# Two gates of a gated block as eight pairs of weight tiles by seven products, results through DRAM

## The chip, the cores and the metric

One Trainium2 chip; the kernel runs on one of its cores. The metric is the device time of one execution in microseconds (us). The core has a matmul engine (PE), a vector engine (DVE), a scalar engine (ACT), a general engine (POOL) and a queue engine (SP) that issues most DMAs. Each runs its own instructions in order, and they wait for each other by semaphores.

## The reference

The input x has 1024 tokens of 1024 channels. All matrices are float32.

```python
h = rmsnorm(x, norm_g)
xa, za, ub, gb, zb, g_a, g_b = split(h @ w_in)          # seven sections of 1024 channels
# first branch: short conv, chunkwise matrix memory with 4 heads, normalization, skip
ya = ((ha + skip_a * xc) * silu(za)) @ w_proj_a
# second branch: 31-tap causal conv, layer norm over channels
c = causal_depthwise_conv(ub * sigmoid(gb), conv_b_w, conv_b_b)
c = standardize(c) * ln_b_g + ln_b_b
yb = (silu(c) * silu(zb)) @ w_pw2 + b_pw2
x = x + (sigmoid(g_a) * ya + sigmoid(g_b) * yb) @ w_out
ple_gate = sigmoid(rmsnorm(x, ple_norm_g) @ w_ple_gate)
return rmsnorm(x + (p @ w_ple) * ple_gate, final_g)
```

## The kernel before

Channels lie on the 128 partitions, tokens on the free axis, so a product is made per output tile: 128 channels by 1024 tokens. Every float32 operand is split exactly into a high part (a cast by ACT to a 22-bit-like format, `split`, line 87) and a low part (the difference, by DVE or POOL, line 88). A product of two operands takes three matmuls: high x high, high x low, low x high. `gemm` (lines 209 to 222) makes one output tile: 8 blocks of the contraction x 2 halves of the tokens x 3 = 48 matmuls of a 128x128 weight and 128x512 moving columns, into one PSUM buffer of the pool `pg` (two buffers, tiles `g`). The other small results use `pm` (four banks, tiles `m`).

Weights come as a stream in a fixed order (`order`, class `Stream`): tile `wr` is loaded by SP into a single buffer, its parts `wh` and `wl` are made by ACT and DVE one tile ahead, with two buffers each. `h` lies in four buffers of the pool `hp` (high and low part of each token half). Long-lived tiles use the pool `sp` (20 buffers, tiles `s`), short ones `zp` (3) and `vp` (4).

The order of the work: p @ w_ple and the rmsnorm; the x section with its short conv; four heads, each with two tiles of za and a chunkwise recurrence; then, for eight tiles t, the first gate's section (`GA + t`) and the first branch's projection (`proj`, t), whose result waits in DRAM (`ma_d`). The long conv of the second branch (31 taps on DVE, line 350) is made of eight tiles, whose taps are drained beside all this in small numbers; each needs two tiles of `in` (sections GB and UB), and its result waits in DRAM (`c_d`). Then six tiles of the second gate (section GBT), the layer norm's sums (lines 636 to 665), two more gate tiles, and eight tiles of the value gate (section ZB), with the activation of the layer norm (`second_act`) two tiles behind. At last the second projection (`pw2`), the merge, and `out` and `gate` by token halves.

Each engine's order is set by a list scheduler when the kernel is built; on the chip the order is fixed.

## Time and profile before

| | |
|---|---|
| time, median of 3 runs | 1172.83 us (1172.17 to 1173.25) |
| profiled execution: span from first to last instruction | 1169.3 us |
| PE matmul busy | 1147.2 us, 98% |
| DVE busy | 817.7 us, 70% |
| ACT busy | 400.4 us, 34% |
| POOL busy | 33.0 us, 3% |
| chain that ended last | PE 93%, DVE 4% |

The span is one profiled execution; the runs' times are some 3.5 us longer, since they hold what lies around it. An engine's busy share says how much of the span it worked, not whether the end waited for it: that is read from the waits of PE and from the chain.

### The profile page before, as it was taken

Reading aid. Unit: us, or ns where it says so; the run is one execution under the profiler, and the core shown is the slowest. Engines: PE = TensorE matmul, PEld = TensorE weight load, DVE = VectorE, ACT = ScalarE, POOL = GpSimd, SP = SyncE. Lnnn points to the kernel's source line nnn. Section 1 sums busy time; section 2 is a strip of 40 time slices with the busy share of each in tenths; the row PEclk is TensorE's granted clock in tenths of the full one; section 3 lists DMA queues with packets and bytes.
Section 4 is the critical chain, followed back from the end, with each engine's and each line's share of the span. In section 5 each row is a group of like instructions: output and inputs, shape, how many; then the busy total and the mean of one; then the engine's idle time right before and its main releaser. Section 6 shows DMA issues by size and latency. Waiting matters only on the chain.

```text
span 1169.3 us, 13098 instructions
## 1 busy us (share of the span) xinstructions
PE 1147.2 (98%) x5276; PEld 929.8 (80%) x5276; DVE 817.7 (70%) x1113; ACT 400.4 (34%) x540; POOL 33.0 (3%) x67
## 2 busy tenths in 40 slices
PE   7999999999999999999999999999999999999996
PEld 5777777778787887888888888888888888888885
DVE  5929989869984699828769999365334545466875
ACT  7633323642525343221111111147232212334542
POOL 1400000000000000000000000000000000000000
PEclk9999999999999999999999999999999999999998
DMA  9311121201011011221211233211113229422232
GB/s 328 133 36 36 38 72 36 71 20 55 19 62 47 19 55 37 72 91 42 102 54 55 108 105 112 90 54 36 55 36 108 90 73 387 152 87 94 91 127 72
DMA packets 29660, 98.18 MB, mean 84 GB/s; under 512 B 3148, under 2 KB 5340, under 8 KB 29600
## 3 DMA queue, kind: packets, MB, share of 16 engines
q1 hardware_dynamic: 25344, 82.37, 20.5%
q0 software_dynamic: 4256, 14.98, 3.3%
q8 instruction: 41, 0.67, 0.2%
q14 instruction: 19, 0.16, 0.0%
HBM read 80.55 MB, written 16.79 MB: 83 GB/s over the span
## 4 chain that ended last, share of the span: by engine, by line
PE 93%; DVE 4%; ACT 1%; DMA 1%; issue 0%; SPq 0%; DVEq 0%; ACTq 0%
PE g L221 21%; PE g L217 21%; PE g L218 21%; PE g L235 5%; PE g L234 5%; PE g L236 5%; PE m L548 2%; PE m L561 2%; PE m L535 1%; PE m L403 1%; PE m L555 1%; PE m L512 1%; DVE s L296 1%; PE m L594 1%; PE m L421 1%; PE m L250 1%
## 5 line engine op out<-in xcount | busy, mean ns | idle before, releaser
L217 PE MATMUL g<-hhi,wh 128*128 128x512 f32 x896 | 354.4, 396 | 0.5 <-ACT s L266 0.5
L218 PE MATMUL g<-hlo,wh 128*128 128x512 f32 x896 | 352.2, 393 | 0.4 <-POOL hlo L88 0.4
L350 DVE SCALAR_TENSOR_TENSOR s<-s,vecs,s 128x1023 f32<-128x1023 f32 (+15 forms) x240 | 300.5, 1265 | 4.3
L221 PE MATMUL g<-hhi,wl 128*128 128x512 f32 x896 | 283.0, 394 | 0.0
L87 ACT CAST wh<-wr 128x1024 fp32r<-128x1024 f32 x72 | 75.8, 1053 | 437.1 <-PE g L218 432.4
L221 PEld LDWEIGHTS g<-hhi,wl 128*128 128x128 f32 x896 | 167.7, 188 | 38.3 <-issue 4.5
L217 PEld LDWEIGHTS g<-hhi,wh 128*128 128x128 f32 x896 | 168.3, 188 | 37.2 <-issue 2.9
L218 PEld LDWEIGHTS g<-hlo,wh 128*128 128x128 f32 x896 | 168.3, 188 | 36.2 <-issue 1.8
L88 DVE TENSOR_TENSOR wl<-wr,wh 128x1024 fp32r<-128x1024 f32 x72 | 87.9, 1220 | 121.4 <-ACT wh L87 121.2
L217 PE MATMUL g<-s,wh 128*128 128x512 f32 x256 | 101.0, 395 | 0.0
L218 PE MATMUL g<-s,wh 128*128 128x512 f32 x256 | 100.8, 394 | 0.0
L221 PE MATMUL g<-s,wl 128*128 128x512 f32 x256 | 80.2, 394 | 0.0
L87 ACT CAST wh<-s 128x1024 fp32r<-128x1024 f32 x32 | 33.6, 1050 | 76.8 <-PE g L235 32.6
L218 PEld LDWEIGHTS g<-s,wh 128*128 128x128 f32 x256 | 48.1, 188 | 11.4
L217 PEld LDWEIGHTS g<-s,wh 128*128 128x128 f32 x256 | 48.1, 188 | 11.3
L221 PEld LDWEIGHTS g<-s,wl 128*128 128x128 f32 x256 | 48.1, 188 | 11.3
L235 PE MATMUL g<-nlo,wh 128*128 128x512 f32 (+1 forms) x136 | 51.5, 379 | 0.0
L234 PE MATMUL g<-nhi,wh 128*128 128x512 f32 (+1 forms) x136 | 51.3, 377 | 0.0
L236 PE MATMUL g<-nhi,wl 128*128 128x512 f32 (+1 forms) x136 | 51.2, 377 | 0.0
L88 DVE TENSOR_TENSOR wl<-s,wh 128x1024 fp32r<-128x1024 f32 x32 | 39.1, 1223 | 16.1 <-ACT wh L87 16.0
L235 PE MATMUL g<-mlo,wh 128*128 128x512 f32 x128 | 50.0, 391 | 0.0
L234 PE MATMUL g<-mhi,wh 128*128 128x512 f32 x128 | 49.8, 389 | 0.0
(193 smaller groups left out, 1340.7 us busy)
## 6 DMA issues: line engine op xcount, KB each, us to landing
wr<-in_w_in SPq DMA_DIRECT2D x56, 512.0 KB, 3.4
s<-in_xT SPq DMA_DIRECT2D x16, 512.0 KB, 9.1
s<-in_w_out SPq DMA_DIRECT2D x16, 512.0 KB, 10.1
s<-in_w_gate SPq DMA_DIRECT2D x16, 512.0 KB, 3.5
ple_d<-s POOLq DMA_DIRECT2D x8, 512.0 KB, 3.8
c_d<-s POOLq DMA_DIRECT2D x8, 512.0 KB, 2.9
wr<-in_w_proj SPq DMA_DIRECT2D x8, 512.0 KB, 3.4
s<-c_d SPq DMA_DIRECT2D x8, 512.0 KB, 4.0
```

Source lines behind the costliest of these rows:

```text
L87: A.copy(out=hi, in_=src)
L88: eng.tensor_tensor(out=lo, in0=src, in1=hi.bitcast(F32), op=ALU.subtract)
L217: PE.matmul(o, hi[:, kt], act_hi(kt, h), start=kt == 0, stop=False)
L218: PE.matmul(o, hi[:, kt], act_lo(kt, h), start=False, stop=False)
L221: PE.matmul(o, lo[:, kt], act_hi(kt, h), start=False, stop=kt == NT - 1)
L234: PE.matmul(ps, hi[:, kt], act_hi(kt)[:, qs], start=kt == 0, stop=False)
L235: PE.matmul(ps, hi[:, kt], act_lo(kt)[:, qs], start=False, stop=False)
L236: PE.matmul(ps, lo[:, kt], act_hi(kt)[:, qs], start=False, stop=kt == NT - 1)
L250: PE.matmul(dst[:, c * P:(c + 1) * P], rcol[:, c:c + 1].broadcast_to([P, P]), ident, start=True, stop=True)
L350: yield lambda d=d: V.scalar_tensor_tensor(out=c[:, d:], in0=ug[:, :S - d], scalar=vcol("conv_b_w", t, KB - 1 - d, KB), in1=c[:, d:], op0= ...
L548: PE.matmul(up, xn[:, i * P:(i + 1) * P], v, start=True, stop=True)
L561: PE.matmul(p2, qt[i][:, cs], X[:, i], start=i == 0, stop=i == 1)
```

## The change

Sections GBT and ZB (16 output tiles) are made as eight pairs of output tiles. The two tiles of a pair, the two halves of the contraction and the two halves of the tokens make 2x2 blocks, and seven products of blocks take the place of eight (Strassen's scheme in Winograd's form). The four sums of the activation's blocks (`quarter_sums`, 16 tiles of `sp` that stay) are made once by POOL from a copy of h in DRAM (`h_d`); the four sums of the weight's blocks and all low parts by POOL for each pair (class `Pair`). PSUM results are combined by DVE (five additions a pair), the gates' results go to DRAM (`gb_d`, `zb_d`). In this stage the order on PE, ACT, DVE and POOL is the written one.

To make room, what the first branch leaves (`u`) and its gate (`ga_d`) wait in DRAM, its projection (`proj`, eight tiles) is moved behind the pairs, beside the layer norm, and reads `u` from the buffers that h had. The weight stream is made in half tiles with four buffers. Results of the long conv are written from SP's queue instead of POOL's.

```diff
-    wp = ctx.enter_context(tc.tile_pool(name="wp", bufs=2))
+    wp = ctx.enter_context(tc.tile_pool(name="wp", bufs=4))
...
+    ma_d, h_d, u_d, ga_d, gb_d, zb_d = [dp.tile([NT, P, S], F32, name=n)
+                                        for n in ("ma_d", "h_d", "u_d", "ga_d", "gb_d", "zb_d")]
...
-                hi = wp.tile([P, NT, P], F32R, tag="wh", name=f"wh{i}")
-                lo = wp.tile([P, NT, P], F32R, tag="wl", name=f"wl{i}")
-                split(raw, hi, lo)
-                self.ready[i] = (hi, lo)
+                two = [weight_parts(raw, f"w{i}_{q}") for q in range(2)]
+                for q, (hi, lo) in enumerate(two):
+                    split(raw[:, q * KH:(q + 1) * KH], hi, lo)
+                self.ready[i] = Halves(two[0][0], two[1][0]), Halves(two[0][1], two[1][1])
...
-        plan("proj", t)
-        if t in (0, 2):
-            plan_pair(6 + t // 2)
-    plan("in", *range(GBT, GBT + NT))
-    plan("in", *range(ZB, ZB + NT))
+        if t in (1, 5):
+            plan_pair(6 + t // 5)
+    first = len(order)
+    plan("proj", *range(NT))
     plan("pw2", *range(NT))
     for kind in ("out", "gate"):
         plan(kind, *range(NT))
         plan(kind, *range(NT))
...
+            nc.sync.dma_start(out=h_d[t][:, h * HT:(h + 1) * HT], in_=x)
...
-        yield lambda: G.dma_start(out=c_d[t], in_=c)
+        yield lambda: nc.sync.dma_start(out=c_d[t], in_=c)
...
-            hi, lo = slot(dt=F32R), slot(dt=F32R)
-            split(xc[2 * h + i], hi, lo)
-            u_hi.append(hi)
-            u_lo.append(lo)
+            nc.sync.dma_start(out=u_d[2 * h + i], in_=xc[2 * h + i])
...
+    def quarter_sums(k):
+        xa_, xb_ = slot(), slot()
+        nc.sync.dma_start(out=xa_, in_=h_d[k])
+        nc.sync.dma_start(out=xb_, in_=h_d[k + KH])
+        s12, s34 = slot(), slot()
+        a0, a1, b0, b1 = xa_[:, :HT], xa_[:, HT:], xb_[:, :HT], xb_[:, HT:]
+        G.tensor_tensor(out=s12[:, :HT], in0=a1, in1=a0, op=ALU.subtract)
+        G.tensor_tensor(out=s12[:, HT:], in0=b1, in1=s12[:, :HT], op=ALU.subtract)
+        G.tensor_tensor(out=s34[:, :HT], in0=a1, in1=b1, op=ALU.subtract)
+        G.tensor_tensor(out=s34[:, HT:], in0=b0, in1=s12[:, HT:], op=ALU.subtract)
+        got = []
+        for q in (s12, s34):
+            hi, lo = slot(dt=F32R), slot(dt=F32R)
+            split(q, hi, lo, G)
+            got.append((hi, lo))
+        tf.append(got)
...
+    for k in range(KH):
+        quarter_sums(k)
     for t in range(NT):
         ps = gemm("in", GA + t, hhi, hlo)
         sg = slot(pool=zp)
         A.activation(sg, ps, AF.Sigmoid)
-        drain(5)
-        ps = gemm("proj", t, tiles_act(u_hi), tiles_act(u_lo))
+        nc.sync.dma_start(out=ga_d[t], in_=sg)
+        drain(9)
+        if t in (1, 5):
+            long_conv(6 + t // 5)
+            drain(9)
...
+        def parts(self, src):
+            uid[0] += 1
+            hi, lo = weight_parts(src, f"s{uid[0]}")
+            split(src, hi, lo, G)
+            return hi, lo
+        def a11(self):
+            self.w1 = self.parts(self.r[0][:, :KH])
+        def a12(self):
+            self.w2 = self.parts(self.r[0][:, KH:])
+        def sums(self):
+            r0, r1 = self.r
+            z = slot((P, NT, P))
+            G.tensor_tensor(out=r1[:, :KH], in0=r1[:, :KH], in1=r0[:, :KH], op=ALU.subtract)
+            G.tensor_tensor(out=z[:, :KH], in0=r1[:, :KH], in1=r1[:, KH:], op=ALU.add)
+            G.tensor_tensor(out=z[:, KH:], in0=z[:, :KH], in1=r0[:, :KH], op=ALU.add)
+            self.z = z
+        def s2(self):
+            self.w6 = self.parts(self.z[:, :KH])
+        def s1(self):
+            self.w5 = self.parts(self.z[:, KH:])
+        def s3(self):
+            self.w7 = self.parts(self.r[1][:, :KH])
+        def s4(self):
+            r0 = self.r[0]
+            G.tensor_tensor(out=r0[:, KH:], in0=r0[:, KH:], in1=self.z[:, :KH], op=ALU.subtract)
+            self.w3 = self.parts(r0[:, KH:])
+        def a22(self):
+            self.w4 = self.parts(self.r[1][:, KH:])
...
+    def product(o, w, f, more=False):
+        for k in range(KH):
+            hi, lo = operand(f, k)
+            PE.matmul(o, w[0][:, k], hi, start=k == 0 and not more, stop=False, skip_group_check=more)
+            PE.matmul(o, w[0][:, k], lo, start=False, stop=False, skip_group_check=more)
+            PE.matmul(o, w[1][:, k], hi, start=False, stop=k == KH - 1, skip_group_check=more)
...
+    def pair(n, w, nx, last):
+        a, b, c, d = banks(n)
+        u = slot(pool=zp)
+        z, u = u[:, HT:], u[:, :HT]
+        out = Out(w)
+        product(a, w.w1, "B11")
+        if last:
+            last()
+        w.s1()
+        drain(1)
+        product(b, w.w6, "T2")
+        A.copy(out=u, in_=a)
+        w.s3()
+        drain(1)
+        product(a, w.w2, "B21", True)
+        V.tensor_tensor(out=u, in0=u, in1=b, op=ALU.add)
+        w.s4()
+        if nx:
+            nx.load()
+        drain(1)
+        product(d, w.w5, "T1")
+        out.put(0, 0, a)
+        w.a22()
+        drain(1)
+        product(c, w.w7, "T3")
+        V.tensor_tensor(out=z, in0=u, in1=d, op=ALU.add)
+        if nx:
+            nx.a11()
+            nx.sums()
+        drain(1)
+        product(d, w.w3, "B22", True)
+        V.tensor_tensor(out=z, in0=z, in1=c, op=ALU.add)
+        out.put(1, 1, z)
+        if nx:
+            nx.s2()
+        drain(1)
+        product(c, w.w4, "T4", True)
+        V.tensor_tensor(out=z, in0=u, in1=d, op=ALU.add)
+        out.put(0, 1, z)
+        if nx:
+            nx.a12()
+        drain(1)
+        def rest():
+            V.tensor_tensor(out=u, in0=u, in1=c, op=ALU.add)
+            out.put(1, 0, u)
+        return rest
+    pairs = [Pair(sec, j) for sec in (GBT, ZB) for j in range(KH)]
...
+    with tc.manual_schedule(engines={mybir.EngineType.PE, mybir.EngineType.Activation,
+                                     mybir.EngineType.DVE, mybir.EngineType.Pool}):
+        last = None
+        for n, w in enumerate(pairs):
+            last = pair(n, w, pairs[n + 1] if n + 1 < len(pairs) else None, last)
+        last()
+        drain()
+    ws.add([srcs[n][t] for n, t in order[first:]])
+    u_hi = [hp.tile([P, NT, HT], F32R, tag="H", name=f"uhi{h}") for h in range(2)]
+    u_lo = [hp.tile([P, NT, HT], F32R, tag="H", name=f"ulo{h}") for h in range(2)]
+    for t in range(NT):
+        u = slot()
+        nc.sync.dma_start(out=u, in_=u_d[t])
+        for h in range(2):
+            split(u[:, h * HT:(h + 1) * HT], u_hi[h][:, t], u_lo[h][:, t], G if h else V)
+    def proj(t):
+        ps = gemm("proj", t, lambda kt, h: u_hi[h][:, kt], lambda kt, h: u_lo[h][:, kt])
+        sg = slot(pool=zp)
+        nc.sync.dma_start(out=sg, in_=ga_d[t])
         V.tensor_tensor(out=sg, in0=ps, in1=sg, op=ALU.mult)
+        nc.sync.dma_start(out=ma_d[t], in_=sg)
+    for t in range(5):
+        proj(t)
...
+        z = slot(pool=vp)
+        nc.sync.dma_start(out=z, in_=zb_d[t])
...
-    LAG = 2
-    for t in range(NT + LAG):
-        if t < NT:
-            ps = gemm("in", ZB + t, hhi, hlo)
-            z = slot()
-            A.activation(z, ps, AF.Silu)
-            szb.append(z)
-        if t >= LAG:
-            second_act(t - LAG)
-    # ---- second branch's projection and the merge ----
+    for t in range(NT):
+        if t < 3:
+            proj(5 + t)
+        second_act(t)
...
-        g = sgb[t]
+        g = slot(pool=zp)
+        nc.sync.dma_start(out=g, in_=gb_d[t])
```

**POOL in the pairs.** Before, this part of POOL's queue holds only DMAs.

```order
L353 DMA c_d<-s_3287 128x1024
L616 DMA ma_d<-s_3720 128x1024
L616 DMA ma_d<-s_3958 128x1024
L616 DMA ma_d<-s_4083 128x1024
L353 DMA c_d<-s_4023 128x1024
```

In the changed kernel POOL has these rows for one pair; `ls` is a low part of weights, `hs` its high part, `s` a raw weight tile or a sum.

```order
L89 TENSOR_TENSOR ls_4858<-s_4791,hs_4857 128x512
L89 TENSOR_TENSOR ls_4876<-s_4750,hs_4875 128x512
L704 TENSOR_TENSOR s_4749<-s_4749,s_4791 128x512
L89 TENSOR_TENSOR ls_4895<-s_4749,hs_4894 128x512
L89 TENSOR_TENSOR ls_4919<-s_4750,hs_4918 128x512
L89 TENSOR_TENSOR ls_4937<-s_4898,hs_4936 128x512
L688 TENSOR_TENSOR s_4899<-s_4899,s_4898 128x512
L689 TENSOR_TENSOR s_4940<-s_4899 128x512
L690 TENSOR_TENSOR s_4940<-s_4940,s_4898 128x512
L89 TENSOR_TENSOR ls_4962<-s_4940,hs_4961 128x512
L89 TENSOR_TENSOR ls_4982<-s_4898,hs_4981 128x512
```

In the same stretch DVE has the additions from PSUM (`s<-s,g` or `s<-s,m`) and the long conv's taps (line 366 now).

```order
L768 TENSOR_TENSOR s_4695<-s_4695,g_4694 128x512
L366 SCALAR_TENSOR_TENSOR s_4608<-s_4113,vecs,s_4608 128x1009
L774 TENSOR_TENSOR s_4695<-s_4695,g_4694 128x512
L366 SCALAR_TENSOR_TENSOR s_4608<-s_4113,vecs,s_4608 128x1008
L781 TENSOR_TENSOR s_4695<-s_4695,g_4694 128x512
L366 SCALAR_TENSOR_TENSOR s_4608<-s_4113,vecs,s_4608 128x1007
L366 SCALAR_TENSOR_TENSOR s_4608<-s_4113,vecs,s_4608 128x1006
L752 TENSOR_TENSOR s_4841<-s_4841,m_4838 128x512
```

The making of low parts for these weights has moved from DVE to POOL, and the sums are new.

**ACT at the end of the last head.** Before, after the head's last scalings (line 562), the two casts of u (line 87, `s<-s`) and the casts of whole weight tiles (`wh`) follow.

```order
L562 ACTIVATE s_3407<-m_3503,cols 128x258
L575 ACTIVATE r_1_3513<-s_3407 128x4
L580 ACT_TABLE_LOAD
L580 ACTIVATE r_1_3513<-r_1_3513,eps_c 128x4
L87 CAST s_3543<-s_1287 128x1024
L87 CAST s_3547<-s_1388 128x1024
L87 CAST wh_3729<-wr_3665 128x1024
L612 ACT_TABLE_LOAD
L612 ACTIVATE s_3720<-g_3671 128x1024
```

In the changed kernel the casts of the quarter sums (`s<-s`, 128x1024, each of which follows POOL) stand between the half weight tiles (`hw`).

```order
L574 ACTIVATE s_3518<-m_3614,cols 128x258
L88 CAST hw_1_3854<-wr_3717 128x512
L587 ACTIVATE r_1_3624<-s_3518 128x4
L88 CAST s_3806<-s_3800 128x1024
L88 CAST s_3810<-s_3801 128x1024
L88 CAST hw_0_3923<-wr_3850 128x512
L592 ACT_TABLE_LOAD
L592 ACTIVATE r_1_3624<-r_1_3624,eps_c 128x4
L88 CAST s_3824<-s_3818 128x1024
L88 CAST s_3828<-s_3819 128x1024
L88 CAST hw_1_3925<-wr_3850 128x512
L654 ACT_TABLE_LOAD
```

The casts of u are gone, and weight casts stand behind casts that wait for POOL: `hw_1_3925` (second half of the second gate tile's weights) behind `s_3828` (a sum of the third quarter).

**PE behind the layer norm's sums.** Before, the row of the layer norm's scale is spread over the partitions (line 250) within the last gate tile (`g_5505`), and the eight tiles of section ZB follow.

```order
L217 MATMUL g_5505<-hhi_272,wh_5444 128x512
L218 MATMUL g_5505<-hlo_274,wh_5444 128x512
L221 MATMUL g_5505<-hhi_271,wl_5445 128x512
L221 MATMUL g_5505<-hhi_272,wl_5445 128x512
L250 MATMUL m_5375<-ident,rl 128x128 x4
L250 MATMUL m_5380<-ident,rl 128x128 x4
L217 MATMUL g_5505<-hhi_271,wh_5444 128x512
```

In the changed kernel it stands within the last tile of the first branch's projection (`g_6490`), of which 38 matmuls are left.

```order
L233 MATMUL g_6490<-ulo_5859,hw_0_6405 128x512
L232 MATMUL g_6490<-uhi_5858,hw_0_6405 128x512
L233 MATMUL g_6490<-ulo_5860,hw_0_6405 128x512
L265 MATMUL m_6316<-ident,rl 128x128 x4
L265 MATMUL m_6321<-ident,rl 128x128 x4
L236 MATMUL g_6490<-uhi_5857,lw_0_6406 128x512
```

Right behind these, PE has the first two tiles of the second projection (`g_6641`, `g_6712`) mixed, so that each takes the activation's tiles (`s_6543`, `s_6544`) as they come.

```order
L232 MATMUL g_6641<-s_6543,hw_0_6482 128x512
L232 MATMUL g_6712<-s_6389,hw_0_6633 128x512
L233 MATMUL g_6641<-s_6544,hw_0_6482 128x512
L233 MATMUL g_6712<-s_6390,hw_0_6633 128x512
L232 MATMUL g_6712<-s_6389,hw_0_6633 128x512
L233 MATMUL g_6712<-s_6390,hw_0_6633 128x512
```

The eight tiles of the value gate, which stood between the scale's row and the second projection, have moved ahead of the layer norm.

## Rows read from the trace of the kernel before

**Rows 1.** The page, engine totals: busy us, share of the span, instructions.

```profile
PE 1147.2 (98%) x5276; PEld 929.8 (80%) x5276; DVE 817.7 (70%) x1113; ACT 400.4 (34%) x540; POOL 33.0 (3%) x67
```

**Rows 2.** The page, 40 slices of the span: PE's granted clock in tenths.

```profile
PEclk9999999999999999999999999999999999999998
```

**Rows 3.** Waits of PE: who for whom, us in total, times, longest.

```profile
PE g L262 <- ACT s L87: 6.7, 2, 6.5
```

**Rows 4.** Timeline of DVE, gates: start, us, operation, [idle before].

```profile
739.27 1.23 DVE L88 TENSOR_TENSOR wl<-wr,wh 128x1024 fp32r<-128x1024 f32 x1 [3.08 <-ACT wh L87]
...
750.15 1.22 DVE L88 TENSOR_TENSOR wl<-wr,wh 128x1024 fp32r<-128x1024 f32 x1 [5.75 <-ACT wh L87]
761.03 1.23 DVE L88 TENSOR_TENSOR wl<-wr,wh 128x1024 fp32r<-128x1024 f32 x1 [9.66 <-ACT wh L87]
```

**Rows 5.** Timeline of POOL, low parts of h.

```profile
39.16 1.68 POOL L88 TENSOR_TENSOR hlo<-s,hhi 128x512 fp32r<-128x512 f32 x1 [0.28 <-ACT hhi L87]
...
43.43 1.68 POOL L88 TENSOR_TENSOR hlo<-s,hhi 128x512 fp32r<-128x512 f32 x1 [0.90 <-ACT hhi L87]
...
45.65 1.31 POOL L88 TENSOR_TENSOR hlo<-s,hhi 128x512 fp32r<-128x512 f32 x1
...
47.72 1.28 POOL L88 TENSOR_TENSOR hlo<-s,hhi 128x512 fp32r<-128x512 f32 x1 [0.24 <-ACT hhi L87]
```

**Rows 6.** Timeline of DVE in the same stretch.

```profile
38.98 0.68 DVE L88 TENSOR_TENSOR hlo<-s,hhi 128x512 fp32r<-128x512 f32 x1
...
40.24 1.14 DVE L88 TENSOR_TENSOR hlo<-s,hhi 128x512 fp32r<-128x512 f32 x1
...
44.54 1.12 DVE L88 TENSOR_TENSOR hlo<-s,hhi 128x512 fp32r<-128x512 f32 x1
```

**Rows 7.** Groups of DVE by shape: count, busy us, mean ns, idle before.

```profile
L88 DVE TENSOR_TENSOR s<-s,s 128x512 fp32r<-128x512 f32 x24 | 15.5, 687 | 6.6 <-ACT s L87 6.5
...
L296 DVE SCALAR_TENSOR_TENSOR s<-s,vecs,m 128x512 f32<-128x512 f32 x16 | 11.2, 738 | 1.3 <-PE m L250 1.3
...
L678 DVE TENSOR_TENSOR s<-s,s 128x512 f32<-128x512 f32 x16 | 10.8, 685 | 0.0
...
L350 DVE SCALAR_TENSOR_TENSOR s<-s,vecs,s 128x1023 f32<-128x1023 f32 x8 | 10.3, 1282 | 0.2
...
L652 DVE TENSOR_TENSOR s<-s,m 128x512 f32<-128x512 f32 x16 | 10.1, 680 | 0.0
...
L676 DVE TENSOR_TENSOR s<-s,m 128x512 f32<-128x512 f32 x16 | 9.7, 679 | 0.6 <-PE m L250 0.6
...
L656 DVE TENSOR_TENSOR s<-s,s 128x1024 f32<-128x1024 f32 x7 | 8.6, 1223 | 1.1 <-ACT s L654 1.1
```

**Rows 8.** Groups of ACT by shape.

```profile
L87 ACT CAST s<-s 128x512 fp32r<-128x512 f32 x24 | 14.0, 617 | 5.7 <-DMA s<-in_w_ple 3.2 <-DVE s L678 1.2 <-DMA s<-in_pT 1.1
...
L87 ACT CAST s<-s 128x1024 fp32r<-128x1024 f32 x8 | 8.3, 1046 | 9.1 <-DVE s L597 9.1
```

**Rows 9.** Timeline of ACT, last head and first gate tile.

```profile
480.37 0.47 ACT L544 ACTIVATE xn<-m,cols 128x256 f32<-128x256 f32 x1 [0.25 <-PE m L542]
...
497.60 1.28 ACT L612 ACT_TABLE_LOAD   x1
498.90 1.03 ACT L612 ACTIVATE s<-g 128x1024 f32<-128x1024 f32 x1
```

**Rows 10.** Timeline of DVE in the last head's end: four scalings.

```profile
489.94 1.39 DVE L586 TENSOR_SCALAR s<-s,r 128x256 f32<-128x256 f32 x4
```

**Rows 11.** Timeline of DVE, end of the layer norm's sums.

```profile
792.23 1.23 DVE L656 TENSOR_TENSOR s<-s,s 128x1024 f32<-128x1024 f32 x1 [1.13 <-ACT s L654]
796.09 0.20 DVE L245 RECIPROCAL rl<-rt 128x8 f32<-128x8 f32 x1 [2.64 <-ACT rt L244]
...
798.84 0.69 DVE L676 TENSOR_TENSOR s<-s,m 128x512 f32<-128x512 f32 x1 [0.35 <-PE m L250]
```

**Rows 12.** Timeline of PE, first products of the span.

```profile
10.14 0.63 PE L264 MATMUL g<-s,s 128*128 128x512 f32 x1
10.57 0.63 PE L262 MATMUL g<-s,s 128*128 128x512 f32 x1
```

More of the change, by code (lines that the diff above doesn't have):

```diff
@@ L27 @@
 EPS = 1e-6
+KH = NT // 2
 CONV_LATER = -2000
@@ L204, in block_kernel @@
     srcs = {"in": w_in, "proj": w_proj, "pw2": w_pw2, "out": w_out, "gate": w_gate}
-    ws.add([srcs[n][t] for n, t in order])
+    ws.add([srcs[n][t] for n, t in order[:first]])
     pos = [0]
```

65 lines of the change are left out of this document (46 added, 19 removed).

## The prediction

> **What bounds the kernel now.** I read the engine totals first: TensorE (PE) is busy for 98% of the span [rows 1]. Its granted clock is full from the first microseconds to the last [rows 2], so no part of that is a slow clock. Then I read the waits of PE: the longest is 6.7 us, at the start, before the first product [rows 3]. So between those ends the other engines cost nothing as long as they deliver in time, and the price of PE's work is its number of matmuls. A weight tile's low part is made once per tile of 48 matmuls, and it comes every 10.87 us [rows 4]: 226.5 ns for one matmul of 512 columns. The profiled execution spans 1169.3 us, and the median of the runs is 1172.83 us, so 3.5 us lie around the span. Differences under 0.2% (2.3 us) cannot be told from no change here.
>
> **Products removed.** Sixteen tiles of 48 matmuls (768) become eight pairs of seven products of 12 matmuls (672). 96 x 226.5 ns = 21.7 us less on PE. A pair takes 84 x 226.5 ns = 19.0 us. The rest of PE's work is the same work in another order. What remains is to see whether PE still waits for nobody, at four places.
>
> **Place 1, the pairs: can GpSimd (POOL) keep up?** Each pair needs seven low parts and four sums, eleven POOL instructions of two 128x512 operands from SBUF; before, POOL issues only DMAs here. The trace has eight of this kind. Alone one takes 1.28 to 1.31 us; where VectorE (DVE) is at its own subtraction of two SBUF operands, 1.68 us, and DVE's becomes 1.12 to 1.14 us instead of 0.68 us [rows 5, 6]. Line them up: the DVE instruction begun at 40.24 us ends at 41.38 us, 0.54 us after the POOL instruction of 39.16 us, and that one ended 1.18 us after the DVE instruction begun at 38.98 us. They take turns. DVE's instructions with one operand in PSUM (line 296) keep their mean of 738 ns beside POOL [rows 7]. So eleven in a row take 11 x 1.28 = 14.1 us, under the 19.0 us of a pair. But DVE has seven taps of the long conv in each pair (50 in all), 1.28 us each with both operands in SBUF [rows 7]. A turn of DVE's 0.68 us instruction costs POOL 0.40 us, so a tap costs about its 1.28 us less the same 0.28 us, 1.0 us. With taps, a pair costs POOL 14.1 + 7.0 = 21.1 us, 2.1 us more than PE needs. Weights are prepared three products ahead (8 us), which hides the first pair only, and the last pair has no successor to prepare: 2.1 x 6 = 12.6, I take 13 us. Bounds: 1 us if a tap does not take turns with POOL, since 14.1 us then fits; 23 us if POOL also stands idle for the cast (0.62 us [rows 8]) once or twice a pair. The taps never meet POOL in the trace of before, so the value rests on DVE's subtractions, the nearest rows.
>
> The Trainium skill (SBUF — State Buffer, section "Who interferes with whom") says that a DVE instruction with two SBUF inputs contends with a GpSimd instruction that reads SBUF, and that the pair of ports is locked for a whole instruction. The rows agree for subtractions (1.68 for 1.28 us). By that rule the taps contend too and this place costs its 13 us; by the rows of POOL alone it would cost 1 us.
>
> **Place 2, before the pairs: the quarter sums.** POOL makes four quarters of four 128x512 sums and two 128x1024 low parts, about 2.5 us each (twice 1.28 less one start). ScalarE (ACT) casts each sum in between, in order, and the casts of PE's next weight tiles stand behind: the second half for the second sigmoid-gate tile stands behind two quarters and the sums of the third. Before, the last scaling of the last head is at 480.37 us and the first gate tile's sigmoid at 498.90 us, behind a table load of 1.28 us [rows 9], so that tile's products end near 497 us. In the changed order the cast of the first quarter follows that scaling, at 481 us; from there POOL needs 2 low parts (5.0), a quarter (5.1 + 5.0) and four sums (5.1), 20.2 us, and ACT two casts of 1.05 us [rows 8]: 503.3 us. The weight's cast and low part add 0.62 + 0.69 us, and DVE's four scalings before PE's transposes 1.39 us [rows 10]: 506 us. PE stands there at 497 + 11 x 0.2265 = 499.5 us and waits 6.5 us. If the seven taps in that stretch all take their 1.0 us from POOL, and the next weight half waits for the fourth quarter, it is 15 to 18 us. I take 10. Bounds 5 (should the casts come earlier) and 18.
>
> **Place 3, into the first projection.** Its operands take the buffers of h, which the pairs read to their last product but one. Casts and low parts of the second token half start only then: eight POOL instructions at 1.28 us and DVE's share, against 2.7 us of the last product and 1.36 us for each step of the first tile. 2 us; bounds 0 and 5.
>
> **Place 4, the layer norm.** Before, ten tiles (two gates, eight value gates) lie beside it and DVE has slack. Now three projection tiles do. From the end of the fifth DVE needs, in its order: 1.9 us of other work, 16 x 0.68 (mean subtracted), 7 x 1.223 (squares summed), three low halves of 0.69 and one product of 1.22 [rows 7, 4]: 24.7 us. PE has two tiles, 21.7 us, and the mean's products, about 1.5 us, and waits 1 us. From the last sum of squares to the first scaled tile it was 798.84 - 793.46 = 5.4 us [rows 11]; PE has nine matmuls before it needs the row: wait 0.6 us. Then eight tiles of activation, 16 x (0.679 + 0.685 + 0.687) = 32.8 us, with four low halves and one product 36.8 us [rows 7], end at 66.9 us. PE would be through the last projection and the first two tiles of the next (96 matmuls, interleaved to follow the activation) at 60 us; it ends 1.4 us behind DVE, a wait of 8.2 us. Then the third tile needs the PSUM buffer that DVE empties after all this, two instructions of 0.75 with three of 0.69 between: 3.6 us. Together 13 us; bounds 8 (emptied beside the last products, fewer waits) and 18.
>
> **Work that costs nothing.** The halves of weights (two casts of 0.62 for one of 1.05 us, two low parts of 0.69 for one of 1.22 us) add 0.35 us to each of the other tiles on ACT and DVE, under 10.87 us of products. The 40 MB of new traffic are spread over stages in which the queues are a quarter busy at most; a load that is late would show at POOL's sums.
>
> **Sum.** 1169.3 - 21.7 + 13 + 10 + 2 + 13 = 1185.6 us of span, and with 3.5 us around it 1189 us.
>
> **Rivals.**
> (B) *Taps do not hold POOL up.* For it: no tap beside POOL in the trace. Against: subtractions of the same two operands do. Then place 1 costs 1 us and place 2 its 6.5: 1172.8 - 21.7 + 1 + 6.5 + 2 + 13 = 1174 us, within 1169 to 1179.
> (C) *Faster: the casts of the sums do not hold the weights up.* One mechanism, at place 2: the quarters are through before PE asks. It decides from a POOL price of two thirds of 1.28 us, or if the first quarters start some 10 us earlier than the scaling; the same POOL then keeps up with the pairs, taps or no taps (21.1 - 14.1/3 = 16.4 us for 19.0). Places 1 and 2 cost 2 us together: 1172.8 - 21.7 + 2 + 2 + 10 = 1165 us. Against it: the rows never show POOL under 1.28 us.
> (D) *Waits that feed themselves.* The array's first matmuls lie 0.43 us apart [rows 12] instead of 0.2265. If PE goes back to that pace after its waits at places 1, 2 and 4, 36 us in all, for as long as they lasted, 36 / 0.43 = 84 matmuls cost 0.2 us more each: 1189 + 17 = 1206 us. The trace has no wait that long after the start.
> The Trainium skill (TensorE: Matmul & The Clock Gate, section "HAM oscillation — how this bites in real kernels") says that an array which waits for data is throttled again and pays for it after each wait. No stretch of the trace of before shows it; by that rule D gains, and I leave it with a small chance since most waits here are single microseconds between products.
>
> **Chances.** The forecast, all four places near their values (1179 to 1202 us): 0.53. B 0.17, C 0.15, D 0.15. C is faster, and a quarter of B; another quarter of B is the same, with a little of the forecast's edge. So faster 0.20, same 0.06, slower 0.74. For 8 in 10 the range reaches to the bulk of C and of D: 1164 to 1209 us. The likeliest case's own is 1179 to 1202 us.
>
> **What would show it.** Place 1: POOL busy almost without a gap in the pairs, its mean well above 1.28 us, taps above 1.28 us, PE waiting for low parts made by POOL; a pair longer than 19.0 us. Place 2: ACT waiting for POOL before the casts of sums, and PE then for weights or transposes. Place 3: PE waiting for the projection's operands for 2 us. Place 4: PE waiting for DVE's low parts at the first two tiles of the second branch's projection, and once for DVE to empty a PSUM buffer. I am wrong if POOL's mean in the pairs stays near 1.28 us with taps beside it, if its casts are early at place 2, or if PE's matmuls lie further apart than 226.5 ns.

## The result and the profile after

| | median of runs (range) | profiled span |
|---|---|---|
| before | 1172.9 us (1172.17 to 1173.25) | 1169.3 us |
| after | 1208.76 us (1208.27 to 1212.4) | 1205.3 us |

The ratio is 1.0315, 95% interval 1.0303 to 1.0328: 36 us slower, where 16 were forecast. The page's totals answer to [rows 1], its clock row to [rows 2]: PE is busy 6.1 us less, although 21.7 us of products are gone, it is idle for more of the span, and the clock has a slice at 0.7.

```profile
PE 1141.1 (95%) x5180; PEld 914.1 (76%) x5180; DVE 890.6 (74%) x1225; ACT 444.4 (37%) x706; POOL 238.2 (20%) x171
PEclk9999999999999999979999999999999999999998
```

The waits of PE after (who for whom, us in total, times, longest); in the kernel before, none behind that of [rows 3] is longer than 2.1 us:

```profile
PE m L606 <- DVE s L598: 19.0, 1, 19.0
...
PE g L717 <- POOL ls L89: 4.1, 2, 2.1
PE g L715 <- DVE s L762: 3.5, 4, 0.9
PE g L715 <- DVE s L768: 3.5, 4, 0.9
PE m L497 <- ACT s L489: 3.0, 1, 3.0
PE g L715 <- ACT s L748: 2.8, 4, 0.7
...
PE m L715 <- DVE s L762: 1.7, 1, 1.7
PE m L715 <- DVE s L768: 1.4, 1, 1.4
```

**Place 2** is the first row: the last head's transposes (L606) wait 19.0 us for the normalization on DVE. DVE's own timeline shows why (start, us, instruction):

```profile
496.32 3.31 DVE L366 SCALAR_TENSOR_TENSOR s<-s,vecs,s 128x1023 f32<-128x1023 f32 x1
499.56 2.35 DVE L590 TENSOR_TENSOR r<-r 128x4 f32<-128x4 f32 x1
501.83 2.38 DVE L366 SCALAR_TENSOR_TENSOR s<-s,vecs,s 128x1022 f32<-128x1022 f32 x1
504.14 1.23 DVE L591 TENSOR_TENSOR r<-r,mv 128x4 f32<-128x4 f32 x1
...
523.25 1.37 DVE L598 TENSOR_SCALAR s<-s,r 128x256 f32<-128x256 f32 x4
```

A multiplication of four elements a partition takes 1.22 to 2.35 us here, and a tap 2.4 to 3.4 us beside POOL (1.26 us twice, 1.28 in [rows 7]). DVE is never idle here: taps and the short instructions of the chain stand in turn behind POOL's quarter sums and their low parts (POOL's timeline after):

```profile
508.74 6.10 POOL L89 TENSOR_TENSOR s<-s,s 128x1024 fp32r<-128x1024 f32 x2
514.79 2.23 POOL L629 TENSOR_TENSOR s<-s 128x512 f32<-128x512 f32 x1
```

The wait brings the lower clock. Busy us of the engines by stretches; the last three columns are granted clock, DMA share and GB/s:

```profile
510.00:515.00 5.00, 0.00 (x0) 0.00 (x0) 5.00 (x3) 2.69 (x3) 5.00 (x3) 0.50 0.00 0
...
525.00:530.00 5.00, 5.00 (x23) 4.26 (x22) 4.88 (x5) 0.62 (x1) 3.77 (x2) 0.83 0.52 188
```

0.50 is 1.2 GHz. It returns to 2.4 GHz some 3 us after PE has work again; matmuls 0.40 to 0.57 us apart until then make about 1.4 us, and place 2 some 20.4 us.

**Place 1**, the pairs, lasts from 643.2 us to the projection's first product at 819.7 us (first and last start of these groups on PE, then their shapes):

```profile
L715 PE MATMUL g<-hhi,hs x48: 387/389/497, 643.2 to 792.1; 128*128 128x512 f32 x48
```

```profile
L232 PE MATMUL g<-uhi,hw x128: 388/389/792, 819.7 to 912.3; 128*128 128x512 f32 x128
```

That is 176.5 us for 152.2 us of products at 226.5 ns: 24.3 us more. Adding up the distances between starts of matmuls beyond 226.5 ns, by what PE waited for: 11.8 us are twelve waits, three in each of the four pairs whose results lie in the two-bank tiles `g` (waits on L762, L768 and L748); 4.4 us are POOL's low parts; 3.5 us are two waits in the last pair (results in `m`); 4.6 us have no wait named: some 1.5 in the matmul right behind each wait (0.31 to 0.34 us), the rest in many that lie 227 to 237 ns apart. DVE's timeline has the same addition in a `g` pair and in an `m` pair:

```profile
658.25 0.69 DVE L762 TENSOR_TENSOR s<-s,g 128x512 f32<-128x512 f32 x1 [1.45 <-PE g L717]
...
677.10 0.69 DVE L762 TENSOR_TENSOR s<-s,m 128x512 f32<-128x512 f32 x1
```

In the `g` pair DVE stood idle until the products into the tile's other half were done; PE's next product then waited for this addition.

**The start**, for which nothing was forecast. By the 94th to 96th of the products with the head's state (L561 before, L573 after) the changed kernel is 5.3 us late (PE's timelines of before and after):

```profile
453.81 0.82 PE L561 MATMUL m<-X,s 128*128 128x258 f32 x3
```

```profile
459.14 0.82 PE L573 MATMUL m<-X,s 128*128 128x258 f32 x3
```

PE's timeline has this in three parts. 2.1 us are there before the heads begin (the matmul ahead of PE's wait for the exponentials starts at 231.92 us, before at 229.85): the first products keep their slow pace for longer (last section). 1.4 us are the wait for the exponentials itself, 3.0 us (L497 above) for

```profile
PE m L481 <- ACT s L473: 1.6, 1, 1.6
```

in the kernel before. And 1.7 us are the lower clock behind it: the eight matmuls that follow (L527) take 5.30 us, before (L512) 3.60 us.

Place 3 shows no wait on the projection's operands. Place 4 shows waits of 5.4 us together, on DVE's reading of PSUM (L884) and on the activation's parts (L88, L89), and the lower clock after them (0.81 and 0.85 in two stretches of 5 us, 1.2 GHz for a part of each). What is left of the 36 us for both is 36 - 5.3 - 20.4 - 24.3 + 21.7 = 7.7 us.

### The profile page after: what moved, and what is told of

It is laid out like the page before. It is cut to its first block, busy times and chain, and to the rows that moved or that the text cites. A ratio compares the mean times of both kernels' runs of the same rounds, so it can differ in the third digit from the quotient of the medians.

```text
span 1205.3 us, 13771 instructions
## 1 busy us (share of the span) xinstructions
PE 1141.1 (95%) x5180; PEld 914.1 (76%) x5180; DVE 890.6 (74%) x1225; ACT 444.4 (37%) x706; POOL 238.2 (20%) x171
## 4 chain that ended last, share of the span: by engine, by line
PE 82%; DVE 6%; POOL 5%; issue 4%; ACT 2%; DMA 1%; SPq 0%; POOLq 0%; DVEq 0%; ACTq 0%
PE g L233 15%; PE g L232 15%; PE g L236 15%; PE g L250 5%; PE g L249 5%; PE g L251 5%; PE m L560 2%; PE m L573 2%; POOL ls L89 2%; PE g L715 2%; DVE s L366 2%; PE g L717 2%; PE g L716 2%; PE m L419 1%; PE m L527 1%
## 5 line engine op out<-in xcount | busy, mean ns | idle before, releaser
L366 DVE SCALAR_TENSOR_TENSOR s<-s,vecs,s 128x1023 f32<-128x1023 f32 (+14 forms) x240 | 342.1, 1425 | 4.1
L232 PE MATMUL g<-hhi,hw 128*128 128x512 f32 x640 | 253.2, 396 | 0.0
L233 PE MATMUL g<-hlo,hw 128*128 128x512 f32 x640 | 252.7, 395 | 0.4 <-POOL hlo L89 0.2
L236 PE MATMUL g<-hhi,lw 128*128 128x512 f32 x640 | 202.3, 394 | 0.0
L88 ACT CAST hw<-wr 128x512 fp32r<-128x512 f32 x112 | 68.5, 619 | 294.0 <-PE g L233 169.3
L233 PEld LDWEIGHTS g<-hlo,hw 128*128 128x128 f32 x640 | 120.4, 188 | 29.5 <-issue 3.7
L232 PEld LDWEIGHTS g<-hhi,hw 128*128 128x128 f32 x640 | 120.5, 188 | 26.5 <-issue 2.8
L236 PEld LDWEIGHTS g<-hhi,lw 128*128 128x128 f32 x640 | 119.8, 188 | 25.0 <-issue 1.1
L89 DVE TENSOR_TENSOR lw<-wr,hw 128x512 fp32r<-128x512 f32 x112 | 80.9, 726 | 58.0 <-ACT hw L88 54.3
L89 POOL TENSOR_TENSOR ls<-s,hs 128x512 fp32r<-128x512 f32 x56 | 93.9, 1694 | 114.9 <-ACT hs L88 114.1
L88 ACT CAST hw<-s 128x512 fp32r<-128x512 f32 x64 | 39.6, 619 | 68.7 <-PE g L250 52.5
L89 DVE TENSOR_TENSOR lw<-s,hw 128x512 fp32r<-128x512 f32 x64 | 44.0, 687 | 23.5 <-ACT hw L88 23.2
L88 ACT CAST hs<-s 128x512 fp32r<-128x512 f32 x56 | 34.2, 615 | 64.1 <-POOL s L704 29.4
L232 PE MATMUL g<-s,hw 128*128 128x512 f32 x128 | 50.5, 402 | 4.7 <-DVE s L884 2.6
L233 PE MATMUL g<-s,hw 128*128 128x512 f32 x128 | 50.5, 402 | 0.7 <-DVE s L89 0.7
```

The lines of the kernel that those rows point to most:

```text
L88: A.copy(out=hi, in_=src)
L89: eng.tensor_tensor(out=lo, in0=src, in1=hi.bitcast(F32), op=ALU.subtract)
L232: PE.matmul(o, hi[:, kt], act_hi(kt, h), start=kt == 0, stop=False)
L233: PE.matmul(o, hi[:, kt], act_lo(kt, h), start=False, stop=False)
L236: PE.matmul(o, lo[:, kt], act_hi(kt, h), start=False, stop=kt == NT - 1)
L366: yield lambda d=d: V.scalar_tensor_tensor(out=c[:, d:], in0=ug[:, :S - d], scalar=vcol("conv_b_w", t, KB - 1 - d, KB), in1=c[:, d:], op0= ...
```

## The experiments

All times are medians; each is to be read against 1208.8 us after and 1172.9 us before.

**One change at a time, first round.** The halves of two-bank tiles given to other results; quarter sums one by one behind gate tiles 2 to 5, with `s12` in the pool `zp`, so that each waits for a gate tile; no copy of h; two projection tiles before the layer norm.

```diff
-        return [q[:, h * HT:(h + 1) * HT] for q in g for h in range(2)]
+        return [q[:, h * HT:(h + 1) * HT] for h in range(2) for q in g]
```

> Theory (a tile is released as a whole): where a pair's four partial results are the halves of two two-bank tiles, an addition that reads one half waits until the products into the other half are done, and the next product into the first half then waits for the addition: three waits in each of four pairs, 11.8 us of gaps between matmuls in all. With a and c in one tile and b and d in the other, no result is read while its tile is written, and the time is 1208.8 - 11.8 = 1197 us; should POOL, 18.9 us a pair, be the next to be late, 1199 to 1203 us. Rival (the additions are late because VectorE stands behind taps that take turns with POOL): the waits stay, 1207 to 1210 us.

1203.97 us. The twelve waits are gone, but 4.4 us of waits for ACT came in their place, and the last pair's wait grew to 6.1 us.

```diff
-        s12, s34 = slot(), slot()
+        s12, s34 = slot(pool=zp), slot()
...
-    for k in range(KH):
-        quarter_sums(k)
...
         drain(9)
+        if 2 <= t <= KH + 1:
+            quarter_sums(t - 2)
```

> Theory (POOL's quarter sums hold VectorE up): with the quarter sums spread behind the first gate's tiles, the last head's normalization finds VectorE's ports free, its small instructions take 0.16 us again instead of 1.2 to 2.4 us, PE's wait of 19.0 us before the head's transposes and the slow clock after it go: 1208.8 - 18 = 1191 us. Rival (the wait is ScalarE's casts standing before the weights, as predicted, about 10 us of it, and VectorE is held up by its own taps): 1199 us, with VectorE's small instructions still above 1 us where taps stand around them.

1206.29 us. The wait of 19.0 us is gone and was given back: PE waited four times, 11.3 us in all, for weights' low parts on DVE (L89), and had the lower clock three times in that stretch. From the 96th product with the head's state to the first pair it takes 181.3 us, where the changed kernel takes 183.7. Spreading POOL's work moved the hold, it did not lift it.

```diff
-            nc.sync.dma_start(out=h_d[t][:, h * HT:(h + 1) * HT], in_=x)
...
-        nc.sync.dma_start(out=xa_, in_=h_d[k])
+        nc.sync.dma_start(out=xa_, in_=xT[k * P:(k + 1) * P, :])
```

> The copy of h is not written; the quarter sums read the input x in its place, so the two gates come out otherwise. Theory (16 writes of 256 KB collide with the loads of the first 50 us): PE's first products of h come 2.6 us earlier, 1208.8 - 2.6 = 1206 us. Rival (the start is late because ScalarE and VectorE make the weights in halves): no change, 1209 us.

1209.29 us: the theory falls. The 4 MB written at the start cost nothing.

```diff
-    for t in range(5):
+    for t in range(2):
         proj(t)
...
-        if t < 3:
-            proj(5 + t)
+        if t < 6:
+            proj(2 + t)
```

> Two tiles of the first projection ahead of the layer norm's sums and six beside the activation, in place of five and three. Theory (the layer norm and the activation need more of VectorE's time than three tiles last): the waits from the last projection to the second tile of the next, 10 us, go: 1199 us. Rival (VectorE can't begin earlier, since the last taps of the long conv and its reload come before): part of it, 1204 us; or the sums now make PE wait instead: 1209 us.

1212.58 us, slower. DVE reads the fourth projection out of PSUM (L813) behind the layer norm's subtractions:

```profile
PE g L232 <- DVE s L813: 7.2, 1, 7.2
```

**Second round: who holds whom.** All of POOL's sums and low parts to DVE (so in each line of `quarter_sums` and `Pair`); the taps left out of the pairs; halves of weights alone, in the kernel before; the results as a with d, b with c.

```diff
-        G.tensor_tensor(out=s12[:, :HT], in0=a1, in1=a0, op=ALU.subtract)
+        V.tensor_tensor(out=s12[:, :HT], in0=a1, in1=a0, op=ALU.subtract)
...
-            split(src, hi, lo, G)
+            split(src, hi, lo)
```

> All of POOL's subtractions and additions (quarter sums, weight sums, low parts) are given to VectorE. Theory (an instruction of POOL holds VectorE up for its whole 1.28 to 2.5 us, where VectorE would do the same work in 0.68 to 1.22 us): the quarter sums take VectorE 21 us in place of some 50 us that it is held up, a pair takes it 20 us of work; the wait of 19.0 us before the head's transposes falls to 2 to 6 us, POOL's 4.4 us in the pairs go, and the time is 1186 to 1194 us. Rival (POOL is of help, and VectorE with 11 more instructions a pair becomes the bound): the pairs take 20 to 22 us each and the time is 1205 to 1220 us.

1194.95 us, 1 us above the theory's range. Place 2 is gone (the first pair starts at 622.1 us, not 643.2), and the pairs give some back: waits on additions in all of them, 18 us.

```diff
         w.s1()
-        drain(1)
```

> The 51 taps of the long conv that stand in the pairs are left out (the conv's result is not whole). Theory (the three waits in each pair on two-bank tiles come from the tile being released as a whole): they stay, 11.8 us; only POOL's lateness goes, with its mean back at 1.28 us: 1208.8 - 4.4 = 1204 us. Rival (the additions are late because of the taps): all of the pairs' waits go, 1208.8 - 16 = 1193 us.

1204.14 us, as the theory has it: the tile waits stay at 11.8 us with no tap beside them, only POOL's go. The groups of POOL in the pairs, after and in this run (count, busy us, mean ns):

```profile
L89 POOL TENSOR_TENSOR ls<-s,hs 128x512 fp32r<-128x512 f32 x55 | 92.0, 1689 | 33.8 <-ACT hs L88 33.0 <-PE m L717 0.7
L690 POOL TENSOR_TENSOR s<-s,s 128x512 f32<-128x512 f32 x7 | 15.8, 2261 | 0.5
```

```profile
L89 POOL TENSOR_TENSOR ls<-s,hs 128x512 fp32r<-128x512 f32 x55 | 70.8, 1297 | 65.5 <-ACT hs L88 65.4
L690 POOL TENSOR_TENSOR s<-s,s 128x512 f32<-128x512 f32 x7 | 9.0, 1293 | 0.5
```

With taps an instruction of POOL takes 1.7 to 2.3 us, without them 1.29 to 1.30. And a tap pays as well (DVE's group of taps after, in the same stretch):

```profile
L366 DVE SCALAR_TENSOR_TENSOR s<-s,vecs,s 128x1018 f32<-128x1018 f32 (+29 forms) x55 | 94.9, 1725 | 0.7
```

The Trainium skill (SBUF — State Buffer, section "Who interferes with whom") says that the pair of ports which DVE shares with GpSimd is an exclusive lock, and that a DVE instruction with two SBUF inputs contends there with a GpSimd instruction that reads SBUF; this case agrees, from both sides.

```diff
-    wp = ctx.enter_context(tc.tile_pool(name="wp", bufs=2))
+    wp = ctx.enter_context(tc.tile_pool(name="wp", bufs=4))
...
-                split(raw, hi, lo)
+                for q, (hi, lo) in enumerate(two):
+                    split(raw[:, q * KH:(q + 1) * KH], hi, lo)
```

> The kernel before, with nothing changed but that weights are made in halves with four buffers. Theory (the 5.7 us that the changed kernel is late already when the last head begins come from the halves, through another order on ScalarE): 1172.8 + 5 = 1178 us, with the wait of PE on ScalarE at the state's exponentials (1.6 us before) at 3 us. Rival (they come from the writes of u, h or the conv, or from the changed order elsewhere): 1173 us.

1178.17 us (ratio 1.0039, 1.0024 to 1.0054): some 5 us come with the halves of weights, and nothing else of the change is needed for the 5.3 us of the start. PE waits 3.0 us for the exponential (L489) here too, where it was 1.6 us before, and in all traces with halves but one the lower clock follows (the stretch behind the wait in the changed kernel, in the kernel before, and in that one, the projection's second run below, with the same wait of 3.0 us):

```profile
236.00:240.00 4.00, 4.00 (x10) 1.82 (x8) 1.67 (x3) 0.91 (x2) 0.00 (x0) 0.57 0.33 132
```

```profile
236.00:240.00 4.00, 4.00 (x21) 3.26 (x20) 1.87 (x3) 3.77 (x11) 0.00 (x0) 1.00 0.01 2
```

```profile
236.00:240.00 4.00, 3.52 (x15) 2.09 (x16) 1.10 (x3) 1.60 (x3) 0.18 (x1) 1.00 0.33 132
```

```diff
-        return [q[:, h * HT:(h + 1) * HT] for q in g for h in range(2)]
+        return [g[0][:, :HT], g[1][:, :HT], g[1][:, HT:], g[0][:, HT:]]
```

> The four partial results are put as a with d and b with c in the two-bank tiles. Theory (whole tiles are released, and with a and c together the third to last product waited for ScalarE's reading of a, 4.4 us): here neither an addition nor that reading falls beside writes to its tile that matter, so both the 11.8 us and the 4.4 us go, and what stays is the last pair (u's low parts ahead of its additions) and POOL: 1198 to 1200 us. Rival (the time is set by POOL at 18.9 us a pair): 1203 to 1205 us as with a and c together.

1203.49 us. The twelve waits and ACT's are gone. What the theory missed: with PE faster, POOL is late, 8.3 us in four pairs (up to 3.0 us), where it was 4.1 us.

**Third round: together.** Quarter sums by DVE (`G` to `V` in `quarter_sums`) with the last banks; the projection again, with this; all three; and fewer taps in the pairs (five for seven, and eleven for nine behind each gate tile).

```diff
-        V.tensor_tensor(out=sg, in0=ps, in1=sg, op=ALU.mult)
+        with tc.high_priority(offset=300):
+            V.tensor_tensor(out=sg, in0=ps, in1=sg, op=ALU.mult)
```

> Quarter sums by VectorE, weight sums and low parts by POOL as in the changed kernel, and the banks as a with d, b with c. Theory (place 2's 20.4 us are POOL's hold on VectorE while the quarter sums run; place 1's tile waits are worth 7.8 us with POOL the next to be late): 1208.8 - 20.4 - 7.8 = 1181 us. Rival (VectorE pays for the quarter sums later in the gate tiles): 1188 us or more.

1179.36 us, as forecast: places 1 and 2 add up.

> Two projection tiles ahead of the layer norm's sums and six beside the activation, as in the attempt that came to 1212.6 us, but VectorE's reading of each projection out of PSUM goes ahead of the layer norm's instructions. Theory (the 7.2 us lost there were PE waiting for that reading behind seven subtractions and squares): the wait goes, and with it the 10 us at the activation: 1200 us. Rival (VectorE's 61.5 us are too long beside what is left of the projection in any order): 1205 to 1210 us.

1201.93 us: the wait on L813 and those at the activation are gone. Place 4 is worth 7 us and is a matter of order.

> All three: quarter sums by VectorE, banks as a with d and b with c, the projection behind two tiles with its reading first. Theory (the three costs stand in different stretches and add): 1208.8 - 20.4 - 7.8 - 9 = 1172 us, as long as the kernel before. Rival (a wait saved in one stretch comes back in the next): 1178 us or more.

1176.4 us (ten runs, 1171.57 to 1179.6; ratio 1.0027, 1.0013 to 1.0041): 3 us for place 4 instead of 9, still behind the kernel before. The profiled execution is the fastest of the ten, and in it the stretch from the projection to the end is as short as in the run before this one (378.1 us; 384.8 us without place 4 mended). What the slower ones lose, and where, no trace shows.

```diff
-        drain(9)
+        drain(11)
```

> As the three together, with five taps of the long conv in a pair in place of seven, and eleven in place of nine behind each gate tile, so that the pairs hold some 31 taps, not 56. Theory (with the banks mended POOL is late by 8 us because taps take turns with it): half of that goes, 4 us less than the three together, 1168 us. Rival (VectorE has no room for more taps beside the gate tiles): 1 to 5 us more than the three together.

1192.63 us. POOL's waits fell to 2.6 us, but DVE had no room beside the gate tiles: taps alone, 25 of them in the rows below, stood ahead of the first pair's first addition, for which PE waited 24.7 us (PE's waits, then DVE's timeline):

```profile
PE g L715 <- DVE s L752: 24.7, 1, 24.7
```

```profile
613.23 42.66 DVE L366 SCALAR_TENSOR_TENSOR s<-s,vecs,s 128x1020 f32<-128x1020 f32 x25
```

**Fourth round: what was still open.** To the three together: two of a pair's low parts by DVE (`a12`, `a22`), and with it the exponentials first. To the kernel after: no taps behind the first two gate tiles; quarter sums by DVE and nothing else. And the three together with the taps in the heads.

```diff
-            self.w2 = self.parts(self.r[0][:, KH:])
+            self.w2 = self.parts(self.r[0][:, KH:], V)
...
-            self.w4 = self.parts(self.r[1][:, KH:])
+            self.w4 = self.parts(self.r[1][:, KH:], V)
```

> The three together, and two of a pair's seven low parts (those of the second half of each raw weight tile) made by VectorE. Theory (POOL is late by 8.5 us in four of the pairs because eleven instructions and the taps' turns come near a pair's 19.0 us): with nine instructions it is on time, 1176.4 - 6 = 1170 us. Rival (VectorE's additions come later and PE waits for them instead): 1175 to 1182 us.

1181.08 us: the rival. POOL is on time, and PE waits 9.8 us for additions (L762) instead, and 3.6 us for a weight's cast behind the pairs. DVE and POOL are now busy alike, 117 of 167 us in the pairs.

```diff
-    A.activation(dec, dec, AF.Exp)
+    with tc.high_priority(offset=400):
+        A.activation(dec, dec, AF.Exp)
```

> As the one with two low parts on VectorE, and the exponentials of the gates (four ScalarE instructions) go ahead of what else ScalarE could do. Theory (of the 5 us that halves of weights cost, some 3 are PE waiting 3.0 in place of 1.6 us for an exponential and a slow clock for 4 us after it): 3 us less than the kernel beside it. Rival (the wait comes from VectorE's chain, ScalarE's order is not it): no difference.

1180.24 us, and the wait of 3.0 us for the exponential is as it was. But this run decides nothing: ScalarE's 706 instructions stand in the same order as without the edit. What the wait hangs on is in the trace of the changed kernel: the last exponential (L489) follows DVE's subtraction L485 at once, and a half tile's low part stands ahead of that one, where the kernel before has none:

```profile
232.40 0.67 DVE L89 TENSOR_TENSOR lw<-wr,hw 128x512 fp32r<-128x512 f32 x1
233.00 1.21 DVE L485 TENSOR_TENSOR s<-mp,s 4x1024 f32<-4x1024 f32 x1
```

That puts L485 back by 0.6 of the 1.4 us; the rest stays open.

```diff
-        drain(9)
+        (skip if t < 2 else drain)(9)
```

> The changed kernel without the 18 taps behind the first two gate tiles (the conv's result is not whole); POOL's quarter sums and ScalarE's casts stay where they are. Theory (taps in turns with POOL are most of place 2): the head's last normalization is done some 10 us after its start in place of 30, PE's wait for it falls from 19.0 to 0 to 4 us, and what stays is the forecast's own cause, 5 to 8 us for weights behind ScalarE's casts: 1208.8 - 13 = 1196 us. Rival (POOL alone holds the small instructions up just as long): PE still waits 12 us or more for the normalization, 1203 us or more.

1208.2 us, and neither theory whole. PE's wait for the normalization fell from 19.0 to 7.2 us (four waits). But POOL alone still holds the small instructions:

```profile
488.39 2.26 DVE L606 TENSOR_TENSOR r<-mv,r 128x4 f32<-128x4 f32 x1
490.69 5.23 DVE L609 TENSOR_SCALAR s<-s,r 128x256 f32<-128x256 f32 x4
```

(the four scalings took 1.39 us in [rows 10]). And the rest came back: 4.3 us for DVE's reading of the next conv's tile (L399), 1.3 us for ACT and a low part, and the lower clock twice. The order of the instructions changed here too, so this run doesn't share out place 2 between taps and small instructions.

> The changed kernel with nothing changed but that the quarter sums and their low parts are made by VectorE. Theory (place 2 is POOL's hold on VectorE in that stretch, whose small instructions and taps take 1 to 3 us each): 1208.8 - 20.4 = 1188 us. Rival (the gain seen so far came from the changed banks): 1200 us or more.

1186.8 us (ratio 1.0120, 1.0103 to 1.0138), as the theory has it. Place 2 by itself is 22 us: whoever makes the quarter sums on POOL pays for them on DVE. The same instructions of DVE here, beside DVE's own quarter sums (L630, L631):

```profile
494.14 0.15 DVE L590 TENSOR_TENSOR r<-r 128x4 f32<-128x4 f32 x1
494.21 0.68 DVE L630 TENSOR_TENSOR s<-s,s 128x512 f32<-128x512 f32 x1
494.82 0.15 DVE L591 TENSOR_TENSOR r<-r,mv 128x4 f32<-128x4 f32 x1
...
503.37 1.38 DVE L598 TENSOR_SCALAR s<-s,r 128x256 f32<-128x256 f32 x4
```

The last kernel is the three together with this in the heads, and three of a pair's seven `drain(1)` left out:

```diff
-                drain(2)
+                drain(3)
```

> The three together, with three taps in place of two for each chunk of the heads, and four in place of seven in a pair, so that 27 taps stay in the pairs and behind them, not 49. Theory (POOL's lateness in the pairs, 8.5 us, comes from the taps' turns, and VectorE is idle for some 45 us in the heads): 1176.4 - 6 = 1170 us, 0.2% under the kernel before. Rival (the heads' own chain on VectorE is held up by the taps): 1176 us or more.

**1160.73 us**, ratio 0.9900 (0.9885 to 0.9914): 12 us faster than the kernel before. The pairs last from 621.0 to 778.2 us, 157.2 us for 152.2 us of products (PE's groups as above), and POOL's waits are one of 0.6 us:

```profile
L715 PE MATMUL g<-hhi,hs x48: 389/389/497, 621.0 to 754.1; 128*128 128x512 f32 x48
```

```profile
L232 PE MATMUL g<-uhi,hw x128: 388/389/477, 778.2 to 873.3; 128*128 128x512 f32 x128
```

The heads took the taps for 1.1 us: from the first to the 96th product with the head's state it is 211.0 us here and 209.9 us in the three together. (The first pair starts at 621.0 us here and at 620.9 us there only because PE's full pace began earlier in this execution; see the last section.) The gain, 15.7 us between the medians, is more than twice what was expected. Between the profiled executions it is 12.1 us, and the pairs alone gave 13.6: some 9 us are POOL's waits, and some 3 us the matmuls at 1.2 GHz behind two of them.

## Why the prediction was wrong

The direction was right. The sizes were not, nor the causes at the two largest places, and one place was missing.

| term | forecast, us | measured, us |
|---|---|---|
| products removed | -21.7 | -21.7 |
| the start, to the last head | 0 | 5.3 |
| place 2, quarter sums | 10 (5 to 18) | 20.4 |
| place 1, pairs | 13 (1 to 23) | 24.3 |
| places 3 and 4 | 15 | 7.7 (what is left) |
| sum | 16.3 | 36.0 |

1208.8 us lies just within the 1164 to 1209 us for 8 in 10, and that is luck: the range reached so far for rival (D), whose mechanism is worth 5 us here.

**Place 2: the step that failed.** "The weight's cast and low part add 0.62 + 0.69 us, and DVE's four scalings before PE's transposes 1.39 us [rows 10]: 506 us": the scalings began at 523.25 us. The prediction had read in [rows 5, 6] that POOL and DVE take turns, and charged the turns to POOL alone. DVE paid more: between the chain's short instructions its queue held taps, and most of both took turns with an instruction of POOL of 1.3 to 3.1 us. ACT's casts, the forecast's own cause, never made PE wait there. With the sums on DVE all of it goes (1186.8 us).

**Place 1: the sum of the wrong things.** POOL's share was near: without taps 11 x 1.295 = 14.2 us a pair (14.1 forecast); with them the mean of its groups in the pairs is 1.77 us, 19.5 us (21.1 forecast: with seven taps a pair, a tap costs POOL some 0.75 us, not 1.0). But PE was late for another reason, a release of two-bank tiles as a whole, 11.8 us. The wait is in the changed kernel's own instruction order: the addition names the tile, and the tile's other half is written just ahead of it. It slowed PE to POOL's pace and so hid most of POOL's lateness, which came out (8.3 us) when it was mended. Rival (B), that taps do not hold POOL up, is refuted by the run without taps.

**The last pair and place 3.** The forecast's 2 us at the projection's first products are not there. u's low parts came earlier, into DVE's queue ahead of the last pair's additions, where they waited for u's loads: 3.5 us, a part of place 1.

**Place 4** was right in kind and too large: 7.7 us with place 3, and 7 us went when order alone was changed.

**Work that costs nothing.** The halves of weights were put at nothing, since they add 0.35 us to a tile "under 10.87 us of products". That was true where products lie ahead, and wrong ahead of the heads, where PE has nothing else: 1.4 us more of a wait and 1.7 us of the lower clock. The row that told of it, PE's wait of 1.6 us on L481, was in the trace of the kernel before; the prediction read the first row of the waits alone (whose 6.7 us are two waits, the longest 6.5 us) and took PE to wait for nobody behind it. The other 2.1 us of the start are the longer slow pace of the first products, which the halves by themselves don't explain.

**Rival (D)** has the right time for the wrong reason. Waits do bring the lower clock (0.50 to 0.57 behind waits of 19.0 and 3.0 us, 0.81 to 0.85 behind 2.6 us), but PE is back at full pace a few us later: about 5 us in the three stretches, not 17. The Trainium skill (TensorE: Matmul & The Clock Gate, section "HAM oscillation — how this bites in real kernels") says that an array that waits for data is throttled again and pays after each wait; the traces agree in kind, but not for each wait (last section). **Rival (C)** failed on both its conditions: no instruction of POOL of 128x512 took less than 1.26 us, and ACT's first casts of sums came right behind the last scaling (483.98 and 483.61 us), not 10 us ahead of it. Its sum also took 10 us for place 4 where the forecast takes 13.

## What to carry to other kernels

When two engines take turns at memory, charge the turn to both, and look first for the short instructions of a chain that PE waits for: a queue of 0.15 us instructions beside the other engine's of 1.3 to 3.1 us becomes a queue of 1.2 to 2.4 us ones. An engine that seems free for sums is not free if its instruction takes twice as long as the busy engine's own and stops that one meanwhile. When partial results share a PSUM tile, put together those that are not read while the other half is written, and after mending one wait look for the one it hid.
